# Latent attention by head pairs: products made one pair ahead, even rows written straight into SBUF, stores begun by three engines

## The chip, the cores and the metric

One core of a Trainium2 chip runs the whole network in one program. The metric is the device time of that program in microseconds (us). The engines are TensorE (PE in the tables; its weight loads are PEld), VectorE (DVE), ScalarE (ACT), GpSimd (POOL) and SyncE (SP, which here only begins DMAs). The trace of the kernel before comes from one profiled execution.

## The reference

Two layers work on 1280 tokens of width 1024 (256 context tokens, 1024 latent ones). A layer projects its input into three groups of heads, mixes them, projects back, and adds a gated convolutional feed-forward block. The change touches the third group, multi-head latent attention with eight heads:

```
cq  = rms_norm(p[9]);   q = cq @ w_uq          # rank 256 -> 8 heads x (64 plain + 32 rotated)
ckv = rms_norm(p[10]);  kn = ckv @ w_uk;  v = ckv @ w_uv     # rank 128 -> 8 heads x 64 each
kr  = p[11]                                    # 32 rotated key columns, one set for all heads
s = (qn . kn + qr . kr) * 96 ** -0.5           # latent queries: 1280 keys; context queries: 256
out = softmax(s) @ v
```

In layer 0 all 1280 tokens are queries, in layer 1 the 1024 latent ones (`lo` in the code is 0 or 256).

## The kernel before

Everything is kept transposed: features on partitions, tokens along the free dimension. Each float32 operand of a large product is split into a rounded high part (a cast on ScalarE, line 212) and a remainder (a subtraction on VectorE, line 213), both fp32r, and a product is three matmuls: high by high, high by low, low by high.

The attention is a Python generator, `mla`. It is woven with a second one, `lin`, which computes the two linear-attention groups: a serial pass over chunk states (lines 594 to 619, `lin_states`), then outputs by group. `weave` takes 1.1 steps of `lin` for each of `mla`, and a scheduler then sets the order of instructions on each engine. The first two steps of `mla` stand at the end of the second projection.

The stage has these parts. `first` makes the split weights, K of head pair 0 (`prod_k`), the rotated query columns of heads 0 to 3 (`prod_qr`), Q of pair 0, V of all heads (`prod_v`, line 872, 512 columns a matmul), and K of pairs 1 to 3. K and Q products (line 885) go through one of three PSUM banks, are split into `t` tiles, and are stored to DRAM (`kq`, line 930); V goes to DRAM too (`vm`, line 875). `load` (lines 942 to 944) then brings one head's K, Q and rotated Q into 96-partition tiles `Kt` and `Q`. While head 0 runs, `rest` makes Q of pairs 1 to 3 and the rotated columns of heads 4 to 7; while head h runs, `following` loads head h + 1.

A head works through query blocks of 128: nine score matmuls of up to 512 keys (`scores`, line 992), maxima on VectorE, exponentials on ScalarE (line 1005), ten transposes on TensorE (`turn`, line 1018), and the product with V (`values`, line 1042), whose normalization needs two diagonal tiles from GpSimd (line 1038). Scores use two sets of three banks in turn; products made meanwhile borrow the three banks of the other set. One output tile per head pair (`ob`) is stored in two pieces to `m` (line 1056). All DMAs are begun by SyncE, which works through its queue in order. Tiles come from pools with a fixed number of buffers: six `t`, sixteen `hid`, eight `h`, eight `y`, four `ws`.

Of the kernel before, what the change touches and what calls it, by code (L numbers as in the profile page):

```python
# [9 lines left out]
F32 = mybir.dt.float32  # L10
# [9 lines left out]
T = 1280  # L20
# [54 lines left out]
class Net:  # L75
# [754 lines left out]
    def mla(self, l, S):  # L830
# [14 lines left out]
        V, Q, ob = {}, {}, {}  # L845
# [6 lines left out]
        def weights():  # L852
            t = [self.hid([128, 512], F32R) for _ in range(2)]
            weight("r", a["uqr"][l].rearrange("p k n -> p (k n)"), [[x[:]] for x in t], 1)
# [10 lines left out]
        def prod_v():  # L865

            t = [self.hid([128, 512], F32R) for _ in range(2)]
# [8 lines left out]
            W.pop("v")  # L876

        def load_v(p):
            V[p] = [self.hid([128, 5, 128]) for _ in range(2)]
            for i in range(2):  # L880
                nc.sync.dma_start(V[p][i][:], S.vm[:, 5 * i:5 * i + 5, 128 * p:128 * p + 128])
# [5 lines left out]
        def prod_qr(x):  # L887

            terms = [(W["r"][wa][0][:, 256 * kc + 128 * x:256 * kc + 128 * x + 128], S.cq[kc][ca]) for kc in range(2) for wa, ca in order]
            for o in range(lo, T, 512):  # L890
# [19 lines left out]
            if x:  # L910
                W.pop("r")

        def prod_k(p):
            hs_ = slice(128 * p, 128 * p + 128)
            to_memory(p, 0, 0, [(W["k"][wa][0][:, hs_], S.ckv[ca]) for wa, ca in order])

        def prod_q(p):
            hs_ = slice(128 * p, 128 * p + 128)
            to_memory(p, 1, lo, [(W["n"][wa][kc][:, hs_], S.cq[kc][ca]) for kc in range(2) for wa, ca in order])

        def to_memory(p, y, o0, terms):

            for o in range(o0, T, 512):
                n = min(512, T - o)
                t = bank()[:, 0:n]
                product(t, o, n, terms)
                hi, lw = self.tt([128, 512], F32R), self.tt([128, 512], F32R)
                self.split(hi[:, 0:n], lw[:, 0:n], t)
                for x, s in enumerate((hi, lw)):
                    nc.sync.dma_start(S.kq[:, p, y, x, o:o + n], s[:, 0:n].bitcast(F32))  # L930
                del hi, lw, s

        def load(h):

            Q[h] = [self.hs([128, T]) for _ in range(2)]
            if h < 2:
                for b in range(2):
                    cs = slice(640 * b, 640 * b + 640)
                    self.split(Kt[h][0][64:96, cs], Kt[h][1][64:96, cs], S.kr[b][64:96, :])
            rows, rot = slice(64 * (h % 2), 64 * (h % 2) + 64), slice(32 * (h % 4), 32 * (h % 4) + 32)  # L940
            for x in range(2):
                nc.sync.dma_start(Kt[h % 2][x][0:64].bitcast(F32), S.kq[rows, h // 2, 0, x])
                nc.sync.dma_start(Q[h][x][0:64, lo:T].bitcast(F32), S.kq[rows, h // 2, 1, x, lo:T])
                nc.sync.dma_start(Q[h][x][64:96, lo:T].bitcast(F32), S.qr[rot, h // 4, x, lo:T])

        def first():
            weights()
            prod_k(0)
            yield
            prod_qr(0)  # L950
            prod_q(0)
            load(0)
            yield
            prod_v()
            yield
            for p in (1, 2, 3):
                prod_k(p)
            load_v(0)
            S.ckv.clear()
            yield  # L960

        def rest():
            load(1)
            S.kr.clear()
            prod_q(1)
            yield
            prod_q(2)
            yield
            prod_qr(1)
            yield  # L970
            prod_q(3)
            S.cq.clear()
            yield

        def following(h):
            load(h)
            if h % 2 == 0:
                load_v(h // 2)
            yield
# [50 lines left out]
        def values(h, qp, pts, sts, nk):  # L1030
# [19 lines left out]
            o = ob[h // 2]  # L1050
            for i in range(2):
                nc.vector.tensor_tensor(o[r:r + 64, 256 * qp + 128 * i:256 * qp + 128 * i + 128],  # L1052
# [5 lines left out]
        for _ in first():  # L1058
            yield
# [473 lines left out]
```

## Time and profile before

| | us |
|---|---|
| median of three runs | 3505.2 |
| lowest and highest run | 3504.65, 3507.97 |
| profiled execution, its own time | 3494.19 |
| its span, first to last instruction | 3492.3 |
| TensorE busy | 3363.4 (96%) |
| VectorE busy | 2225.3 (64%) |
| ScalarE busy | 1549.2 (44%) |
| GpSimd busy | 399.4 (11%) |

Read it as an account of TensorE: what it does in order, and between which instructions it is idle. A wait is put down to the instruction that ended it. Rows of SyncE give the time for which beginning a DMA holds its queue, not the transfer.

### The profile page before, as it was taken

To read this page: it belongs to the slowest core of one execution; us is meant where nothing else is said; L and a number is where in the kernel's file an instruction comes from. 1 tells how busy PE (TensorE), PEld (TensorE's weight loads), DVE (VectorE), ACT (ScalarE), POOL (GpSimd) and SP (SyncE) were. 2 spreads that over 40 slices of the span, in tenths; PEclk is the share of its full clock that TensorE was granted. 3 is DMA by queue.
4 is the path that set the end of the run, shared out by engine and by line. 5 is a ranking of instruction groups with operands and counts; after the bars stand their busy time and mean duration, and the time that the engine had idled before them with its cause. 6 is when DMAs were issued, how large, how long until landed. Compare 5 with 4: busy or idle time off the path is not lost.

```text
span 3492.3 us, 58230 instructions
## 1 busy us (share of the span) xinstructions
PE 3363.4 (96%) x23310; PEld 2932.7 (84%) x23310; DVE 2225.3 (64%) x3797; ACT 1549.2 (44%) x2881; POOL 399.4 (11%) x627
## 2 busy tenths in 40 slices
PE   8997899999999999999999998899999999999998
PEld 6996677678999999999999997577777888888897
DVE  3434678876774444675557844688877765586555
ACT  3333555554453332343334543555554544345433
POOL 0000244441010000000000000134310010001001
PEclk9998899999999999999999998899999999999999
DMA  7656522234223333432223445532234333223321
GB/s 291 202 176 199 200 77 77 62 92 145 73 73 117 119 121 126 152 103 73 79 73 117 168 135 180 188 84 78 57 101 127 99 94 97 92 95 115 96 92 49
DMA packets 207311, 410.01 MB, mean 117 GB/s; under 512 B 18176, under 2 KB 108096, under 8 KB 207040
## 3 DMA queue, kind: packets, MB, share of 16 engines
q1 hardware_dynamic: 207040, 406.29, 36.8%
q8 instruction: 183, 3.00, 0.4%
q14 instruction: 88, 0.72, 0.1%
HBM read 339.90 MB, written 66.32 MB: 116 GB/s over the span
## 4 chain that ended last, share of the span: by engine, by line
PE 84%; DVE 8%; DMA 3%; ACT 2%; issue 2%; SPq 0%; POOL 0%; DVEq 0%; POOLq 0%; ACTq 0%
PE ps L323 45%; PE ps L1242 16%; PE ps L992 5%; PE ps L1042 3%; PE ps L1018 3%; PE ps L457 3%; PE ps L263 1%; PE ps L647 1%; DVE sm L994 1%; DVE hid L707 1%; PE ps L651 1%; PE ps L885 1%; DMA ws<-in_ada_dram 1%; DVE hid L697 1%; ACT w L1005 1%
## 5 line engine op out<-in xcount | busy, mean ns | idle before, releaser
L323 PE MATMUL ps<-h,w 128*128 128x320 f32 (+5 forms) x9600 | 1664.8, 334 | 12.8 <-ACT h L212 6.3
L323 PEld LDWEIGHTS ps<-h,w 128*128 128x128 f32 x9600 | 1530.6, 189 | 144.2 <-issue 7.1
L213 DVE TENSOR_TENSOR w<-ws,w 128x1024 fp32r<-128x1024 f32 x360 | 441.1, 1226 | 564.7 <-PE ps L323 288.6
L1242 PE MATMUL ps<-hid,w 128*128 128x256 f32 (+4 forms) x3696 | 577.2, 316 | 1.5 <-ACT hid L212 1.4
L1242 PEld LDWEIGHTS ps<-hid,w 128*128 128x128 f32 x3696 | 539.6, 189 | 36.0 <-issue 7.6
L212 ACT CAST w<-ws 128x1024 fp32r<-128x1024 f32 x360 | 379.0, 1054 | 419.5 <-PE ps L1242 291.6
L992 PE MATMUL ps<-h,h 96*128 96x512 f32 (+1 forms) x1200 | 330.3, 395 | 31.6 <-DVE w L1020 11.3
L992 PEld LDWEIGHTS ps<-h,h 96*128 96x128 f32 x1200 | 198.7, 194 | 89.3 <-issue 21.5
L1209 DVE SCALAR_TENSOR_TENSOR t<-u,vec,t 128x642 f32<-128x642 f32 (+3 forms) x176 | 144.6, 822 | 181.6 <-ACT t L1208 181.5
L1203 ACT COPY u<-ps 128x512 f32<-128x512 f32 (+4 forms) x264 | 118.3, 483 | 312.1 <-PE ps L323 312.1
L1005 ACT ACTIVATE w<-ps,sm 128x768 f32<-128x768 f32 (+2 forms) x272 | 208.6, 773 | 101.9 <-DVE sm L1001 78.3
L1247 DVE SCALAR_TENSOR_TENSOR y<-ps,mod,y 128x320 f32<-128x320 f32 (+5 forms) x376 | 197.2, 558 | 68.1 <-PE ps L1242 67.7
L1018 PE MATMUL ps<-ident,w 128*128 128x128 f32 x1312 | 224.7, 287 | 13.1 <-ACT w L1005 12.8
L1038 POOL TENSOR_SCALAR dg<-ident,sm 128x128 f32<-128x128 f32 x144 | 98.9, 690 | 995.0 <-DVE sm L1036 906.4
L1018 PEld LDWEIGHTS ps<-ident,w 128*128 128x128 f32 x1312 | 155.0, 144 | 66.9 <-issue 29.1
L1199 POOL MEMSET u<- 128x1 f32 (+1 forms) x264 | 20.8, 102 | 1613.8 <-DVE t L1210 1436.3
L1042 PE MATMUL ps<-w,hid 128*64 128x128 f32 x2624 | 195.2, 282 | 7.3 <-DVE y L1052 7.1
L994 DVE TENSOR_REDUCE sm<-ps 128x1 f32<-128x1024 f32 x128 | 156.3, 1222 | 58.4 <-PE ps L992 48.4
L1042 PEld LDWEIGHTS ps<-w,hid 128*64 128x64 f32 x2624 | 150.5, 138 | 47.2 <-issue 29.1
L1022 ACT COPY w<-ps 128x256 f32<-128x256 f32 (+1 forms) x272 | 128.0, 473 | 109.4 <-PE ps L1018 106.6
L720 POOL TENSOR_TENSOR hid<-hid,hid 128x512 f32<-128x512 f32 x108 | 147.3, 1381 | 68.1 <-ACT hid L700 48.0
L1208 ACT ACTIVATE t<-u,vec 128x642 f32<-128x642 f32 (+3 forms) x176 | 153.6, 872 | 0.4
(197 smaller groups left out, 3231.8 us busy)
## 6 DMA issues: line engine op xcount, KB each, us to landing
ws<-in_up_dram SPq DMA_DIRECT2D x176, 512.0 KB, 3.6
ws<-in_down_dram SPq DMA_DIRECT2D x88, 512.0 KB, 3.4
ws<-in_ada_dram SPq DMA_DIRECT2D x80, 512.0 KB, 4.9
ws<-in_w_in_dram SPq DMA_DIRECT2D x48, 512.0 KB, 4.3
kq<-t SPq DMA_DIRECT2D x64, 256.0 KB, 2.5
ws<-in_w_out_dram SPq DMA_DIRECT2D x32, 512.0 KB, 3.7
h<-kq SPq DMA_DIRECT2D x48, 320.0 KB, 5.2
y<-in_ada_dram SPq DMA_DIRECT2D x16, 512.0 KB, 8.2
```

The costliest lines, as they stand in the source:

```text
L212: self.nc.scalar.copy(hi, src)
L213: self.nc.vector.tensor_tensor(lo, src, hi.bitcast(F32), op=ALU.subtract)
L323: nc.tensor.matmul(ps[:, i, 0:n], w_[:, k, :], h[k][:, part, o:o + n], start=(k == 0 and q == 0), stop=(k == 7 and q == 2))
L720: nc.gpsimd.tensor_tensor(X[n][:], blk(E[n][:, 0, cs[i]]), qx[:], op=ALU.mult)
L992: nc.tensor.matmul(sc[:, o:o + n], q[qa][0:96, qs], K[ka][0:96, o:o + n], start=(x == 0), stop=(x == 2))
L994: nc.vector.tensor_reduce(st[:, 1:2], sc[:, 0:1024], axis=AX.X, op=ALU.max)
L1005: nc.scalar.activation(P[:, c0:c1], sc[:, c0:c1], AF.Exp, bias=st[:, 2:3], scale=MSCALE, accum_out=st[:, 3 + j:4 + j])
L1018: nc.tensor.transpose(ps[:, t_], P[:, 128 * (t0 + t_):128 * (t0 + t_) + 128], self.ident[:])
L1042: nc.tensor.matmul(op[64 * i:64 * i + 64, 0], V[h // 2][t_ // 5][:, t_ % 5, r:r + 64], pts[i][:, t_], start=(t_ == 0), stop=(t_ == nk - 1) ...
L1208: nc.scalar.activation(v[:, 0:n], u[:, 1:1 + n], AF.Identity, scale=cw(j, 1), bias=self.vec[l][:, V_CB + j:V_CB + j + 1])
L1242: nc.tensor.matmul(pb[i][:, 0:n], w[w_][:, x, ms], p.hh[f0 + x][hp][:, o - 1:o - 1 + n], start=(x == 0 and q == 0), stop=(x == gn - 1 and ...
L1247: nc.vector.scalar_tensor_tensor(t, pb[i][:, o:o + n], self.md(l, 5, m, who), t, op0=ALU.mult, op1=ALU.add)
```

## The change

K, Q and V of a head pair are now made while the odd head before that pair runs (pair 0 ahead of head 0), each in a step of its own: `prod_kq` (two steps) and `prod_v` (one). The product tile of a pair has the even head's 64 rows on top and the odd head's below. The top half goes by DMA straight into the even head's `Kt[0]` or `Q` tile, and the bottom half to DRAM, from where `load` brings it during the even head. The high parts' DMAs are begun by ScalarE, the remainders' by GpSimd. V of a pair is computed as ten 128x128 blocks into three banks and copied into its SBUF tiles, with no trip through DRAM. The weights of `prod_qr` and `prod_v` are loaded and split by 128 columns (`some`). Outputs go to a `t` tile for each head and 256 queries, and each is stored at once by SyncE. The diff, with `...` where lines are left out:

```diff
-        def prod_v():
-
-            t = [self.hid([128, 512], F32R) for _ in range(2)]
-            weight("v", a["ukv"][l][:, 1], [[x[:]] for x in t], 1)
+        def some(src, n):
+
+            raw, t = self.tt([128, n, 128]), self.hid([128, 2, n, 128], F32R)
+            nc.sync.dma_start(raw[:], src)
+            self.split(t[:, 0], t[:, 1], raw[:])
+            return t
+
+        def prod_v(p):
+            w = some(a["ukv"][l][:, 1:2, 128 * p:128 * p + 128], 1)
+            V[p] = [self.hid([128, 5, 128]) for _ in range(2)]
+            b = flip[0] ^ 3
+            ps = self.ps[:, b:b + 3, :].rearrange("p a b -> p (a b)")
             for t_ in range(10):
-                p = bank()
                 for x, (wa, ca) in enumerate(order):
-                    nc.tensor.matmul(p, S.ckv[ca][:, 128 * t_:128 * t_ + 128], W["v"][wa][0], start=(x == 0), stop=(x == 2))
-                s = self.tt([128, 512])
-                nc.scalar.copy(s[:], p)
-                nc.sync.dma_start(S.vm[:, t_, :], s[:])
...
+                    nc.tensor.matmul(ps[:, 128 * t_:128 * t_ + 128], S.ckv[ca][:, 128 * t_:128 * t_ + 128], w[:, wa, 0],
+                                     start=(x == 0), stop=(x == 2))
             for i in range(2):
-                nc.sync.dma_start(V[p][i][:], S.vm[:, 5 * i:5 * i + 5, 128 * p:128 * p + 128])
+                nc.scalar.copy(V[p][i][:].rearrange("p a b -> p (a b)"), ps[:, 640 * i:640 * i + 640])
+            yield
...
-                for y, s in enumerate((hi, raw)):
-                    nc.sync.dma_start(S.qr[:, x, y, o:o + n], s[:, 0:n].bitcast(F32))
+                for y, (s, eng) in enumerate(((hi, nc.scalar), (raw, nc.gpsimd))):
+                    eng.dma_start(S.qr[:, x, y, o:o + n], s[:, 0:n].bitcast(F32))
...
+        def prod_kq(p):
+
+            h = 2 * p
+            Q[h] = [self.hs([128, T]) for _ in range(2)]
...
+            turned(h)
             hs_ = slice(128 * p, 128 * p + 128)
+            for y in range(2):
...
+                for o in range(lo if y else 0, T, 512):
+                    n = min(512, T - o)
+                    t = bank()[:, 0:n]
+                    product(t, o, n, terms)
+                    parts = [self.tt([128, 512], F32R) for _ in range(2)]
+                    self.split(parts[0][:, 0:n], parts[1][:, 0:n], t)
+                    for x, (s, eng) in enumerate(zip(parts, (nc.scalar, nc.gpsimd))):
+                        eng.dma_start((Q[h] if y else Kt[0])[x][0:64, o:o + n].bitcast(F32), s[0:64, 0:n].bitcast(F32))
+                        eng.dma_start(S.kq[:, p, y, x, o:o + n], s[64:128, 0:n].bitcast(F32))
+                    del parts, s
+                yield
+
+        def load(p):
+
+            h = 2 * p + 1
             Q[h] = [self.hs([128, T]) for _ in range(2)]
...
+                nc.sync.dma_start(Kt[1][x][0:64].bitcast(F32), S.kq[:, p, 0, x])
+                nc.sync.dma_start(Q[h][x][0:64, lo:T].bitcast(F32), S.kq[:, p, 1, x, lo:T])
...
-            if h % 2 and qp in (2, 4):
-                c0, c1 = (lo, 768) if qp == 2 else (768, T)
-                nc.sync.dma_start(S.m[:, 4 + h // 2, c0:c1], o[:, c0:c1])
...
+            nc.sync.dma_start(S.m[r:r + 64, 4 + h // 2, 256 * qp:256 * qp + 256], o[r:r + 64])
...
+        weights()
+        for _ in chain(prod_qr(0), prod_kq(0), prod_v(0)):
             yield
...
             if h % 2 == 0:
-                ob[h // 2] = self.yk()
-            side = rest() if h == 0 else following(h + 1) if h < 7 else iter(())
+                side = load(h // 2)
+            elif h < 7:
+                p = (h + 1) // 2
+                side = chain(*[prod_qr(1)] * (p == 2), prod_kq(p), prod_v(p))
```

How instructions move, in three places of layer 0. First TensorE, where V's products end. Before, these rows are the last V product (`L872`, all eight heads wide), the rest of a chunk of the linear attention's states (`L612`), and K of pair 1 (`L885`, `y` being the compressed keys and `ws` the weights):

```order
L872 MATMUL ps<-hid_3155,y_374 128x512
L612 MATMUL ps<-hid_3135,hid_3152 32x64 x4
L885 MATMUL ps<-y_374,ws_2576 128x512
L885 MATMUL ps<-y_375,ws_2576 128x512
L885 MATMUL ps<-y_374,ws_2576 128x512 x2
L885 MATMUL ps<-y_375,ws_2576 128x512
L885 MATMUL ps<-y_374,ws_2576 128x512
L885 MATMUL ps<-y_374,ws_2576 128x256
```

Now the end of V's products of pair 0 alone (`L877`) is followed at once by scores of head 0 (`L968`, which was line 992):

```order
L877 MATMUL ps<-hid_3185,y_374 128x128
L877 MATMUL ps<-hid_3185,y_373 128x128
L968 MATMUL ps<-h_2565,h_2709 128x256
L968 MATMUL ps<-h_2565,h_2710 128x256
L968 MATMUL ps<-h_2566,h_2709 128x256
L968 MATMUL ps<-h_2565,h_2709 128x512
L968 MATMUL ps<-h_2565,h_2710 128x512
L968 MATMUL ps<-h_2566,h_2709 128x512
```

K of pair 1 has gone from here into head 1.

Then ScalarE. Before, in head 0, the casts of the products (`L212`) stand by themselves among exponentials (`L1005`), chunk work (`L734`, `L700`, `L703`) and copies of transposes (`L1022`):

```order
L212 CAST t_3714<-hid_3703 128x256
L212 CAST t_3806<-ps 128x512
L212 CAST t_3818<-ps 128x512
L212 CAST t_3830<-ps 128x256
L1005 ACTIVATE w_3754,sm_3719<-ps,sm_3719 128x512
L1005 ACTIVATE w_3754,sm_3719<-ps,sm_3719 128x768
L734 COPY t_3911<-ps 128x512
L700 ACTIVATE hid_4047<-hid_4046 128x2x64x2
L703 ACTIVATE hid_4047<-hid_4046 128x64x2
L1022 COPY w_3846<-ps 128x512
L703 ACTIVATE hid_4047<-hid_4046 128x64x2
```

Now, in head 1, two DMAs stand behind each cast, one into the even head's tile (`L942`) and one to DRAM (`L943`); `L981` is the exponentials, `L998` the copies of transposes:

```order
L981 ACTIVATE w_3943,sm_3900<-ps,sm_3900 128x512
L981 ACTIVATE w_3943,sm_3900<-ps,sm_3900 128x768
L212 CAST t_3975<-ps 128x512
L998 COPY w_4015<-ps 128x512
L942 DMA h_2565<-t_3975 64x512
L943 DMA kq_372<-t_3975 64x512
L212 CAST t_3986<-ps 128x512
L653 COPY hid_4021<-ps 128x2x128
L942 DMA h_2565<-t_3986 64x512
L943 DMA kq_372<-t_3986 64x512
L212 CAST t_3997<-ps 128x256
L998 COPY w_4015<-ps 128x256
```

Up to the next exponential there are eight DMAs in this place.

Last GpSimd. Before, in the same part of the stage, it holds diagonal tiles (`L1038`, for the normalization) and the linear attention's products (`L716`, `L720`, `L803`) only:

```order
L1038 TENSOR_SCALAR dg_4082<-ident,sm_3836 128x128
L1038 TENSOR_SCALAR dg_4086<-ident,sm_3893 128x128
L1038 TENSOR_SCALAR dg_4157<-ident,sm_3963 128x128
L1038 TENSOR_SCALAR dg_4161<-ident,sm_4041 128x128
L716 TENSOR_TENSOR hid_4209<-u_3738,hm 128x512
L720 TENSOR_TENSOR hid_4219<-hid_4010,hid_4209 128x512
L720 TENSOR_TENSOR hid_4237<-hid_4036,hid_4209 128x512
L1038 TENSOR_SCALAR dg_4291<-ident,sm_4103 128x128
```

Now, in head 1, twelve DMAs stand between two pairs of diagonal tiles (`L1014`). The six for K are left out here; these are the six for Q, and what stands behind them:

```order
L942 DMA h_3969<-t_4082 64x512
L943 DMA kq_372<-t_4082 64x512
L942 DMA h_3969<-t_4096 64x512
L943 DMA kq_372<-t_4096 64x512
L942 DMA h_3969<-t_4110 64x256
L943 DMA kq_372<-t_4110 64x256
L1014 TENSOR_SCALAR dg_4255<-ident,sm_3900 128x128
```

The diagonal tile in the last row now comes behind the remainders of a whole pair's K and Q.

## Rows read from the trace of the kernel before

**Rows 1.** The page, parts 1 and 2: busy time by engine; granted clock in 40 slices

```profile
PE 3363.4 (96%) x23310; PEld 2932.7 (84%) x23310; DVE 2225.3 (64%) x3797; ACT 1549.2 (44%) x2881; POOL 399.4 (11%) x627
...
PEclk9998899999999999999999998899999999999999
```

**Rows 2.** Stretches of 100 us; columns: stretch, length, busy time (count) by engine, clock, DMA

```profile
500.00:600.00 100.00, 96.33 (x848) 73.39 (x847) 80.88 (x177) 56.20 (x148) 44.21 (x45) 0.95 0.18 50
...
2400.00:2500.00 100.00, 94.94 (x847) 73.28 (x845) 84.43 (x169) 55.87 (x144) 36.66 (x35) 0.98 0.29 78
```

**Rows 3.** Stretches of 10 us around the first heads of both layers

```profile
330.00:340.00 10.00, 4.93 (x99) 3.53 (x88) 2.43 (x6) 2.70 (x10) 0.00 (x0) 0.50 1.07 220
...
400.00:410.00 10.00, 5.39 (x51) 3.60 (x51) 9.16 (x15) 2.74 (x7) 7.80 (x6) 0.83 0.56 177
410.00:420.00 10.00, 6.56 (x19) 5.06 (x20) 7.99 (x16) 5.51 (x15) 0.60 (x1) 0.52 0.57 195
...
2220.00:2230.00 10.00, 9.39 (x72) 7.80 (x73) 5.90 (x15) 7.27 (x21) 1.20 (x2) 0.69 0.62 201
```

**Rows 4.** Waits of TensorE from 354 to 420 us: total, times, longest

```profile
PE ps L992 <- DVE t L901: 6.2, 2, 4.0
PE ps L992 <- DVE t L213: 3.4, 3, 1.9
PE ps L885 <- DVE t L213: 1.6, 3, 0.8
```

**Rows 5.** Waits of TensorE from 2204 to 2264 us

```profile
PE ps L885 <- DVE t L213: 2.4, 4, 0.9
PE ps L992 <- DVE t L213: 1.7, 3, 0.7
PE ps L885 <- DVE w L1020: 0.8, 1, 0.8
PE ps L992 <- DVE t L901: 0.7, 1, 0.7
```

**Rows 6.** Groups by line and shape, TensorE: busy us, mean ns, idle before

```profile
L457 PE MATMUL ps<-w,h 128*128 128x256 f32 x960 | 116.7, 281 | 0.0
...
L647 PE MATMUL ps<-hid,hid 128*128 128x128 f32 x272 | 47.3, 293 | 1.9 <-DVE hid L640 1.8
...
L872 PE MATMUL ps<-hid,y 128*128 128x512 f32 x60 | 17.1, 449 | 0.0
```

**Rows 7.** TensorE in order of time, four transposes and a single one: start, length

```profile
705.56 0.27 PE L1018 MATMUL ps<-ident,w 128*128 128x128 f32 x1
...
709.03 0.60 PE L1018 MATMUL ps<-ident,w 128*128 128x128 f32 x4
```

**Rows 8.** SyncE's issues of line 930: ns least, median, most

```profile
L930 SPq DMA_DIRECT2D kq<-t x88: 319/398/1816, 282.2 to 2268.4; - x88
```

**Rows 9.** What the transposes' weight loads (line 1018) waited for: us, times

```profile
  ACT w L1005: 21.3, 29
```

**Rows 10.** The page, part 5: a tensor operation on GpSimd

```profile
L720 POOL TENSOR_TENSOR hid<-hid,hid 128x512 f32<-128x512 f32 x108 | 147.3, 1381 | 68.1 <-ACT hid L700 48.0
```

**Rows 11.** SyncE's queue, layer 0, around the first head's loads

```profile
306.97 4.46 SPq L930 DMA_DIRECT2D kq<-t  x6
...
316.20 0.42 SPq L471 DMA_DIRECT2D gqk<-t  x1
316.67 0.43 SPq L588 DMA_DIRECT2D hid<-gqk  x1
```

**Rows 12.** ScalarE at the data of that store

```profile
312.14 0.44 ACT L469 ACTIVATE t<-ps 128x320 f32<-128x320 f32 x1
```

**Rows 13.** TensorE at head 0's first scores and the states' next chunk

```profile
321.52 0.66 PE L992 MATMUL ps<-h,h 96*128 96x256 f32 x2 [2.26 <-DMA h<-qr]
323.21 1.12 PE L604 MATMUL ps<-ident,hid 128*128 128x128 f32 x4 [1.03 <-DVE hid L597]
```

**Rows 14.** ScalarE, 500 to 800 us: exponentials of full score blocks

```profile
L1005 ACT ACTIVATE w<-ps,sm 128x768 f32<-128x768 f32 x43 | 38.5, 895 | 0.0
```

More of the change, by code (lines that the diff above doesn't have):

```diff
@@ L852, in weights @@
         def weights():
-            t = [self.hid([128, 512], F32R) for _ in range(2)]
-            weight("r", a["uqr"][l].rearrange("p k n -> p (k n)"), [[x[:]] for x in t], 1)
             t = self.ws([128, 2, 512], F32R)
@@ L887, in prod_qr @@
         def prod_qr(x):
-            terms = [(W["r"][wa][0][:, 256 * kc + 128 * x:256 * kc + 128 * x + 128], S.cq[kc][ca]) for kc in range(2) for wa, ca in order]
+            w = some(a["uqr"][l][:, :, 128 * x:128 * x + 128], 2)
+            terms = [(w[:, wa, kc], S.cq[kc][ca]) for kc in range(2) for wa, ca in order]
             for o in range(lo, T, 512):
@@ L917, in prod_q @@
[L917 to L931, printed above, removed]
@@ L946, in first @@
[L946 to L973, printed above, removed]
@@ L975, in following, with turned @@
[L975 to L978, printed above, removed]
+            del w, terms
+            yield
+        def turned(h):
+            for x in range(2):
+                nc.sync.dma_start(Q[h][x][64:96, lo:T].bitcast(F32), S.qr[32 * (h % 4):32 * (h % 4) + 32, h // 4, x, lo:T])
+        def prod_kq(p):
+            h = 2 * p
+            Q[h] = [self.hs([128, T]) for _ in range(2)]
+            if p == 0:
+                for K in Kt:
+                    for b in range(2):
+                        cs = slice(640 * b, 640 * b + 640)
+                        self.split(K[0][64:96, cs], K[1][64:96, cs], S.kr[b][64:96, :])
+                S.kr.clear()
+            turned(h)
+            hs_ = slice(128 * p, 128 * p + 128)
+            for y in range(2):
+                if y:
+                    terms = [(W["n"][wa][kc][:, hs_], S.cq[kc][ca]) for kc in range(2) for wa, ca in order]
+                else:
+                    terms = [(W["k"][wa][0][:, hs_], S.ckv[ca]) for wa, ca in order]
+                for o in range(lo if y else 0, T, 512):
[8 more added lines that the diff above has]
+                    del parts, s
+                yield
@@ L1049, in values, with chain @@
             nc.scalar.copy(rb[:], op[:, 1])
-            o = ob[h // 2]
+            o = self.tt([128, 256])
             for i in range(2):
-                nc.vector.tensor_tensor(o[r:r + 64, 256 * qp + 128 * i:256 * qp + 128 * i + 128],
+                nc.vector.tensor_tensor(o[r:r + 64, 128 * i:128 * i + 128],
                                         op[64 * i:64 * i + 64, 0], rb[64 * i:64 * i + 64, :], op=ALU.mult)
-            if h % 2 and qp in (2, 4):
-                c0, c1 = (lo, 768) if qp == 2 else (768, T)
-                nc.sync.dma_start(S.m[:, 4 + h // 2, c0:c1], o[:, c0:c1])
-        for _ in first():
+            nc.sync.dma_start(S.m[r:r + 64, 4 + h // 2, 256 * qp:256 * qp + 256], o[r:r + 64])
+        def chain(*gs):
+            for g in gs:
+                yield from g
+        weights()
+        for _ in chain(prod_qr(0), prod_kq(0), prod_v(0)):
             yield
@@ L1348 @@
         S.qr = net.dp.tile([128, 2, 2, T], F32, name=f"qr{l}")
-        S.kq = net.dp.tile([128, 4, 2, 2, T], F32, name=f"kq{l}")
-        S.vm = net.dp.tile([128, 10, 512], F32, name=f"vm{l}")
+        S.kq = net.dp.tile([64, 4, 2, 2, T], F32, name=f"kq{l}")
         S.ckv = [net.yk(F32R) for _ in range(2)]
```

21 lines of the change are left out of this document (3 added, 18 removed).

## The prediction

> **What bounds the kernel now.** Read the page's busy line and its clock line first: TensorE is busy 96% of the span, ScalarE 44%, GpSimd 11%, and the granted clock leaves its upper level (2.4 GHz) in only a few slices [rows 1]. So the time is TensorE's work plus what it loses, and a change that keeps its matmuls moves the time only through lost stretches, or through what a matmul costs. The table by stretches says what bounds the attention stage, the only one touched: in a typical 100 us of it TensorE is 96% busy, VectorE 80%, ScalarE 56%, GpSimd 44% in layer 0 and 37% in layer 1 [rows 2]. The 10 us slices show where TensorE loses most: while the linear attention's states go round serially (330 to 340 us: 4.9 of 10 us busy, clock 0.50), and again where head 0 runs beside the other pairs' products (410 to 420 us, and 2220 to 2230 us with its clock at 0.69) [rows 3]. The waits of TensorE in those second stretches name the cause: VectorE's splits and rotations (lines 213, 901), with VectorE itself 9.2 of 10 us busy from 400 to 410 us [rows 3 to 5].
>
> **The change, part by part.** The sum is made against the profiled execution (3494.2 us); the three timed runs have their median 11 us above it, and I add the same difference to both.
>
> *V products.* Before, 60 matmuls of 512 columns (30 a layer) take 17.1 us, 0.285 us each [rows 6]. Now there are 240 of 128 columns, each with its own weight load. The trace has no fp32r matmul of 128 columns. Its nearest rows: 960 fp32r matmuls of 256 columns at 116.7/960 = 0.122 us, half of which, 0.061, is the price if time follows columns alone; four transposes of 128 columns end 0.60 us after the first begins, against a single one's 0.27 us, so one each 0.11 us; and plain f32 records of 128 columns take 47.3/272 = 0.174 us [rows 6, 7]. I take 0.115 us, next to the transposes and to the 256-column row, because a weight load of 128 columns stands in front of each: 240 x 0.115 = 27.6, so +10.5 us. Ends: 240 x 0.061 = 14.6 (-2.5) and 240 x 0.174 = 41.8 (+24.7). The Trainium skill's "TensorE: Matmul & The Clock Gate", section "Back-to-back issue gap", gives about 81 ns for sustained matmul and weight-load pairs of 128 columns; by that the term would be an estimated +2.3 us, but the 256-column row here stands 0.015 us above its columns' share, so I stay with the rows.
>
> *Products moved.* K and Q of pairs 1 to 3 and the second rotation (7 steps a layer) leave the stretch around head 0 and go, in the same number of matmuls, into heads 1, 3 and 5, where V's products of those pairs join them: 10 steps a layer. In the old places their splits cost TensorE 6.2 + 3.4 + 1.6 = 11.2 us in layer 0 and 2.4 + 1.7 + 0.8 + 0.7 = 5.6 us in layer 1 [rows 4, 5]: 16.8 us for 14 steps, 1.2 us each. These waits go; late next in the same banks are the splits in the new places. There VectorE is 80% busy and not 92%, so I take 0.9 us: 20 x 0.9 = 18.0, net +1. Ends: nothing at all (-17), or 1.6 us a step, layer 0's price (+15). The clock comes back too: at 0.83 and 0.52 over 5.4 and 6.6 busy us, and at 0.69 over 9.4 [rows 3], the old stretches lost 0.9 + 3.1 + 2.9 = 7 us. I book -7; 0 if the new place cools it as much.
>
> *ScalarE begins 98 stores* (54 in layer 0, 44 in layer 1). On SyncE such an issue holds the queue 0.32 us at least, 0.40 at the median and 1.8 at most [rows 8]. 27 of them fall ahead of the heads, beside projections and states; 71 stand between the exponentials of heads 1, 3 and 5: 71 x 0.40 = 28 us of ScalarE. Each waits for ScalarE's own cast, so the exponentials behind it wait too, and the transposes behind those. ScalarE's 44% of idle time hides the rest, but in 29 of the 144 score blocks (80 in layer 0, 64 in layer 1) the transposes' weight loads already stood waiting for an exponential [rows 9]. So I charge 29/144 of 28 us: +6. Ends 0 and 28.
>
> *GpSimd begins 98 more.* No row of before has one. The nearest are SyncE's 0.40 us and a 128x512 tensor operation on GpSimd, 1.38 us [rows 8, 10]: 71 x (0.40 to 1.38) = 28 to 98 us of an engine that is over half idle. Behind them wait the diagonal tiles (line 1038) that the end of a head's values needs, and the split tiles' six buffers. I take +4, ends 0 and 53 (the second rival).
>
> *The start.* SyncE's queue: six K/Q stores from 306.97 us, six loads, and only at 316.20 us the store of gqk, whose data ScalarE had finished at 312.58 us; its reload is issued at 316.67 us [rows 11, 12]. That holds up the states' next chunk at 323.21 us [rows 13]. With the stores and even rows gone, three loads still stand ahead of it. I take -2 a layer, -4 in all; ends 0 and -7. It can't be more, since TensorE's own queue waits for the rotated rows until 321.52 us anyway [rows 13], and they still go through memory.
>
> *Outputs and the rest.* 72 small output stores replace 16 large ones: 56 more issues of 0.40 us on SyncE, which loses 88 K/Q stores, 20 stores and 16 loads of V. Costed at nothing: SyncE's queue has room. If that cover goes, the output tiles hold the same six buffers as the splits, and VectorE waits.
>
> Sum: +10.5 + 1 - 7 + 6 + 4 - 4 = **+10.5 us**: 3505 us in a profiled execution, and 3505.2 + 10.5, about **3516 us**, as the median.
>
> **Rivals.** *The start gets short.* Around head 0 the products went through three banks with VectorE nearly full; without them head 0 may run like a later head. Then the 16.8 us of waits and 7 us of clock do not come back, since the scheduler has transposes and linear attention to put behind each product, ScalarE's issues hide in its idle time, and the start's -4 holds: -17 - 7 - 4 + 10.5 = -17.5, **3488 us**. For it: VectorE's load in the heads is lower than at 400 us. Against: one engine order runs both, and 10 steps now stand where 7 stood.
>
> *GpSimd runs late.* A pair's two product steps bring 12 issues within two score blocks; 43 full blocks in 300 us make a block 7.0 us [rows 14], so 14 us, of which GpSimd already uses 44%, 6.2 us. Above (14 - 6.2)/12 = 0.65 us an issue, stores fall behind, the split tiles stay held, and products, banks and scores follow. At 1.38 us it is 12 x 1.38 - 7.8 = 8.8 us a pair, six pairs, 53 us; if the blocks behind catch up half, +26 in place of my +4: **3538 us**. The Trainium skill's "SBUF — State Buffer", section "SBUF: two separate sides", speaks for it: descriptors of a transfer begun by GpSimd are written by GpSimd, and a VectorE copy in its two-port mode locks it out. No run here shows that, and most VectorE work of these heads reads PSUM.
>
> *Nothing measurable:* a V product at 0.061 us, ScalarE's issues hidden, steps and clock even: within a few us of 3505.
>
> **How the numbers follow.** Chances: the forecast (above +7 us) 0.38, GpSimd late 0.13, short start 0.31, nothing 0.18. About 0.2% (7 us) is what a measurement of this kernel can tell from no change. So slower 0.51, same 0.18, faster 0.31. The range goes from the short start, with a little more, to the late GpSimd, with half of V's upper end: 3484 to 3550; the forecast's own is 3512 to 3530.
>
> **What would show it.** V's matmuls (new line 877) at 0.11 to 0.12 us each, 240 of them, confirm the largest term; under 0.07 or over 0.17 refutes it. TensorE's waits on line 213's splits should appear in heads 1, 3 and 5 and be gone around head 0, where the clock should stay up. ScalarE's queue should show about 0.4 us an issue, and the transposes' waits for exponentials should grow past 21 us and 29 times. If GpSimd's issues exceed 0.65 us and matmuls wait for its tiles or diagonals, the second rival is at work. The forecast is wrong if the attention stretches of both layers get shorter in sum.

## The result and the profile after

The changed kernel takes 3546.97 us as a median (3539.91 to 3550.99, 4 runs), and the kernel before, measured beside it, 3504.93 us: 1.0117 of before, 95% interval 1.0098 to 1.0135. So it is 42 us slower, where 10.5 were forecast. In the profiled executions the span grows by 54.7 us, from 3492.3 to 3547.0. The 12.6 us between the two figures are no work: the profiled execution of before was 10.7 us quicker than its median, that of the changed kernel 1.9 us slower than its own. What follows is told against the profiles, one execution of each kernel.

The page of the changed kernel, its busy line, its clock line and its DMA queues (q1 is begun by SyncE, q10 by ScalarE, q0 by GpSimd):

```profile
span 3547.0 us, 58820 instructions
...
PE 3408.4 (96%) x23490; PEld 2977.6 (84%) x23490; DVE 2217.4 (63%) x3805; ACT 1548.7 (44%) x2885; POOL 448.2 (13%) x725
...
PEclk9997998999999999999999998899899999999999
...
q1 hardware_dynamic: 180672, 361.19, 32.7%
q10 hardware_dynamic: 8480, 12.33, 1.2%
q0 software_dynamic: 4576, 12.33, 1.2%
```

Against [rows 1], TensorE is busy 45.0 us longer and idle only 9.7 us longer. A longer busy time has two sources: more work, or the same work at the lower clock. They are told apart with the granted clock: over slices of some 10 us, busy time times (1 - clock) is what the lower level took. That sum is 45.2 us before and 76.8 us after. So the 54.7 us are **9.7 of idle time, 31.6 lost to the lower clock, and 13.4 of work**. (In slices of 100 us both sums come out some 15 us higher, and they differ by 30.6.) By place: 18.6 us up to the end of layer 0's attention and 31.6 in layer 1's; most of the other 4.5 us stand behind the last matmul of the program, where 12.2 us have become 16.6, and are idle time of TensorE in code that the change did not touch.

How much of this is chance between two executions, the other runs can say, since each has its mean granted clock. Span times (1 - clock), idle time included, is 70 us in the profiled execution of before and 106 in that of the changed kernel, 36 more. Over all runs on record it averages 74 to 76 us before (four sets of runs) and 98 for the changed kernel: some 24 us more, beside a slowdown of 42. So the lower clock is no accident of one execution, but the two profiles make it look larger than it is.

Three stretches of 100 us of the changed kernel (columns as in [rows 2]; the clock stands behind the engines), and the last two of them in the kernel before; its first is in [rows 2]:

```profile
500.00:600.00 100.00, 90.46 (x655) 68.53 (x654) 66.94 (x143) 45.25 (x115) 33.38 (x42) 0.88 0.28 81
2200.00:2300.00 100.00, 88.41 (x856) 69.21 (x856) 66.00 (x158) 50.62 (x144) 30.64 (x34) 0.82 0.24 67
2500.00:2600.00 100.00, 92.60 (x719) 70.69 (x718) 67.20 (x144) 46.51 (x117) 35.57 (x44) 0.86 0.40 120
```

```profile
2200.00:2300.00 100.00, 90.97 (x760) 68.38 (x759) 73.58 (x163) 55.06 (x143) 29.73 (x29) 0.97 0.57 184
...
2500.00:2600.00 100.00, 96.18 (x854) 73.67 (x855) 79.49 (x175) 55.85 (x139) 31.31 (x40) 0.98 0.29 92
```

VectorE and ScalarE are busy for less of the time than before, GpSimd for about as much, and the clock is 0.82 to 0.88 and not 0.95 to 0.98: TensorE is not held up by a fuller engine; it is idle for somewhat longer, and does its own work slower. Where, the groups by line say (busy us, mean ns | idle before), first for the scores, the transposes, the product with V and V's own products of the changed kernel, then for the first three before:

```profile
L968 PE MATMUL ps<-h,h 96*128 96x512 f32 (+1 forms) x1200 | 339.8, 404 | 32.1 <-DVE t L213 10.7 <-DVE w L996 8.3 <-DMA h<-t 5.3
...
L994 PE MATMUL ps<-ident,w 128*128 128x128 f32 x1312 | 228.0, 291 | 13.9 <-ACT w L981 13.7
...
L1018 PE MATMUL ps<-w,hid 128*64 128x128 f32 x2624 | 206.0, 286 | 8.5 <-DVE t L1028 5.9 <-ACT w L998 2.1
...
L877 PE MATMUL ps<-hid,y 128*128 128x128 f32 x240 | 43.9, 362 | 0.6 <-DVE hid L213 0.6
```

```profile
L992 PE MATMUL ps<-h,h 96*128 96x512 f32 (+1 forms) x1200 | 330.3, 395 | 31.6 <-DVE w L1020 11.3 <-DVE t L901 6.9 <-DVE t L213 5.1
...
L1018 PE MATMUL ps<-ident,w 128*128 128x128 f32 x1312 | 224.7, 287 | 13.1 <-ACT w L1005 12.8
...
L1042 PE MATMUL ps<-w,hid 128*64 128x128 f32 x2624 | 195.2, 282 | 7.3 <-DVE y L1052 7.1
```

V's products (line 877) take 43.9 us for 240, 0.183 us each, 26.8 us more than the 17.1 of [rows 6]. Line 877 alone, in windows around five of its eight batches (TensorE busy and count, weight loads, clock, DMA share, GB/s):

```profile
339.00:349.00 10.00, 6.66 (x30) 6.47 (x30) 0.50 0.20 62
430.00:440.00 10.00, 3.78 (x30) 3.50 (x30) 1.00 0.01 2
700.00:710.00 10.00, 3.46 (x30) 3.50 (x30) 0.85 0.16 43
2440.00:2450.00 10.00, 6.80 (x30) 6.55 (x30) 0.52 0.05 11
2558.00:2568.00 10.00, 6.66 (x30) 6.48 (x30) 0.50 0.17 51
```

A batch of 30 takes 3.5 to 3.8 us at the upper level, 0.115 to 0.126 us each, and 6.7 to 6.8 us at the lower, 0.222 to 0.227. (The clock column is that of the whole window: in the third row it rose before the batch began.) Three batches of eight meet the upper level (from 431, 705 and 2311 us), five the lower, one of these (from 575 us, 6.3 us) for most of its length. How a batch gets there, the stretch around the last one shows (all engines, columns as in the three rows of 100 us):

```profile
2548.00:2558.00 10.00, 5.28 (x28) 3.67 (x28) 5.68 (x9) 4.78 (x15) 5.26 (x7) 0.58 0.85 295
2558.00:2568.00 10.00, 10.00 (x45) 8.55 (x42) 1.63 (x4) 2.13 (x5) 1.37 (x2) 0.50 0.17 51
2568.00:2578.00 10.00, 10.00 (x68) 7.86 (x66) 6.64 (x15) 2.48 (x6) 5.02 (x5) 0.55 0.34 109
```

First TensorE idles 4.7 of 10 us and the clock falls to its lower level; then V's step follows, and TensorE is busy without a gap for 20 us at 0.50 to 0.55. Read in slices of 2 us, the changed kernel has 16 low stretches between 0 and 1000 and between 1900 and 2700 us, and the slice ahead of each had TensorE idle for 0.8 to 2.0 us. The five that meet a V batch last 12 to 46 us, most others 4 to 8.

What TensorE waited for, over the whole span (us in total, times, longest):

```profile
PE ps L994 <- ACT w L981: 13.7, 13, 4.0
PE ps L968 <- DVE t L213: 10.7, 9, 2.8
PE ps L604 <- DVE hid L597: 9.1, 4, 3.1
...
PE ps L612 <- ACT hid L606: 8.3, 13, 0.7
PE ps L604 <- DVE hid L599: 8.2, 7, 1.9
```

The splits (line 213) are waited for nine times; 10.5 of these 10.7 us lie in the four stretches 526 to 580, 676 to 716, 2424 to 2464 and 2534 to 2590 us, in heads 3 and 5. Around head 0, where [rows 4, 5] stood full of them, there is none.

The store issues (min/median/max ns), first on ScalarE, then on GpSimd, for the even rows and for the DRAM copy:

```profile
L942 ACTq DMA_DIRECT2D h<-t x44: 468/468/1425, 303.1 to 2545.5; - x44
...
L942 POOL DMA_DIRECT2D h<-t x44: 516/518/595, 304.1 to 2547.5; - x44
...
L943 ACTq DMA_DIRECT2D kq<-t x44: 453/609/1070, 298.6 to 2549.5; - x44
L943 POOL DMA_DIRECT2D kq<-t x44: 532/532/552, 299.6 to 2548.0; - x44
```

One place shows how such stores can hold up TensorE all the same (timeline: start, duration, engine, line; in brackets the idle time before and what ended it):

```profile
688.42 1.03 POOL L716 TENSOR_TENSOR hid<-u,hm 128x512 f32<-128x512 f32 x1
689.52 1.27 POOL L720 TENSOR_TENSOR hid<-hid,hid 128x512 f32<-128x512 f32 x1
690.74 0.58 POOL L942 DMA_DIRECT2D h<-t  x1
691.32 0.54 POOL L943 DMA_DIRECT2D kq<-t  x1
...
693.24 0.37 ACT L212 CAST t<-ps 128x256 fp32r<-128x256 f32 x1 [5.14 <-DMA kq<-t]
...
693.64 0.42 DVE L213 TENSOR_TENSOR t<-ps,t 128x256 fp32r<-128x256 f32 x1 [3.19 <-ACT t L212]
694.12 1.65 PE L968 MATMUL ps<-h,h 96*128 96x512 f32 x3 [2.85 <-DVE t L213]
```

GpSimd's two stores stand behind 2.3 us of its tensor work; the next cast has no free split tile until a store has landed, VectorE waits for the cast, and the scores for VectorE. The issue itself (0.54 to 0.58 us) is not what is late: the stores begin late, behind that work.

### The profile page after: what moved, and what is told of

Its sections match the earlier page's. It is cut to its first block, busy times and chain, and to the rows that moved or that the text cites. A ratio compares the mean times of both kernels' runs of the same rounds, so it can differ in the third digit from the quotient of the medians.

```text
span 3547.0 us, 58820 instructions
## 1 busy us (share of the span) xinstructions
PE 3408.4 (96%) x23490; PEld 2977.6 (84%) x23490; DVE 2217.4 (63%) x3805; ACT 1548.7 (44%) x2885; POOL 448.2 (13%) x725
## 4 chain that ended last, share of the span: by engine, by line
PE 85%; DVE 6%; DMA 3%; issue 2%; ACT 2%; POOL 0%; SPq 0%; ACTq 0%; DVEq 0%; POOLq 0%
PE ps L323 44%; PE ps L1224 15%; PE ps L968 5%; PE ps L1018 4%; PE ps L994 3%; PE ps L457 3%; PE ps L877 1%; PE ps L885 1%; PE ps L647 1%; PE ps L263 1%; DVE sm L970 1%; PE ps L651 1%; DMA ws<-in_ada_dram 1%; PE ps L354 1%; DVE hid L707 1%
## 5 line engine op out<-in xcount | busy, mean ns | idle before, releaser
L212 ACT CAST w<-ws 128x1024 fp32r<-128x1024 f32 x360 | 379.1, 1054 | 418.6 <-PE ps L1224 291.5
L968 PE MATMUL ps<-h,h 96*128 96x512 f32 (+1 forms) x1200 | 339.8, 404 | 32.1 <-DVE t L213 10.7
L968 PEld LDWEIGHTS ps<-h,h 96*128 96x128 f32 x1200 | 207.3, 202 | 90.2 <-issue 20.2
L1191 DVE SCALAR_TENSOR_TENSOR t<-u,vec,t 128x642 f32<-128x642 f32 (+3 forms) x176 | 144.6, 821 | 182.5 <-ACT t L1190 182.4
L981 ACT ACTIVATE w<-ps,sm 128x768 f32<-128x768 f32 (+2 forms) x272 | 209.0, 774 | 105.1 <-DVE sm L977 80.2
L1018 PE MATMUL ps<-w,hid 128*64 128x128 f32 x2624 | 206.0, 286 | 8.5 <-DVE t L1028 5.9
L998 ACT COPY w<-ps 128x256 f32<-128x256 f32 (+1 forms) x272 | 128.0, 474 | 120.3 <-PE ps L994 116.6
L720 POOL TENSOR_TENSOR hid<-hid,hid 128x512 f32<-128x512 f32 x108 | 144.2, 1352 | 86.4 <-ACT hid L700 58.6
L212 ACT CAST hid<-t 128x642 fp32r<-128x642 f32 (+5 forms) x100 | 63.5, 635 | 207.7 <-DVE t L1196 204.8
```

Of the source, the lines that this page charges most:

```text
L212: self.nc.scalar.copy(hi, src)
L968: nc.tensor.matmul(sc[:, o:o + n], q[qa][0:96, qs], K[ka][0:96, o:o + n], start=(x == 0), stop=(x == 2))
L981: nc.scalar.activation(P[:, c0:c1], sc[:, c0:c1], AF.Exp, bias=st[:, 2:3], scale=MSCALE, accum_out=st[:, 3 + j:4 + j])
L1018: nc.tensor.matmul(op[64 * i:64 * i + 64, 0], V[h // 2][t_ // 5][:, t_ % 5, r:r + 64], pts[i][:, t_], start=(t_ == 0), stop=(t_ == nk - 1) ...
L1191: nc.vector.scalar_tensor_tensor(v[:, 0:n], u[:, 0:n], cw(j, 0), v[:, 0:n], op0=ALU.mult, op1=ALU.add)
```

## The experiments

Theory A: V's thin products cost what the clock makes of them, and the odd heads, where they stand, are where the clock falls. Rivals: B, the stores of ScalarE and GpSimd; C, the K and Q products' own stalls. Ratios are to the kernel before, with 95% intervals; the split into idle, lower clock and work is that of one profiled execution each, worked out as above, and executions of one kernel lie up to 15 us apart. The last column is span times (1 - granted clock) as the mean of all runs of the kernel on record, which is the surer sign of the clock. The work column is coarse: five kernels with the same matmuls (before, V put back with either stores, stores alone, outputs alone) lie between 3311.8 and 3323.7.

| kernel | ratio | span | idle | lower clock | work | all runs |
|---|---|---|---|---|---|---|
| before | 1 | 3492.3 | 128.9 | 45.2 | 3318.2 | 74 to 76 |
| changed | 1.0117 | 3547.0 | 138.6 | 76.8 | 3331.6 | 98 |
| V put back | 1.0030 | 3504.7 | 136.4 | 44.6 | 3323.7 | 75 |
| V ahead of K, Q | 1.0156 | 3548.2 | 144.3 | 62.7 | 3341.2 | 93 |
| V alone on before | 1.0047 | 3514.8 | 130.6 | 48.6 | 3335.6 | 74 |
| V in even heads | 1.0042 | 3509.7 | 128.5 | 42.5 | 3338.7 | 74 |
| steps spaced | 1.0114 | 3540.4 | 144.6 | 52.1 | 3343.7 | 79 |

**V put back.** In the changed kernel V is made as before: 512 columns, through DRAM.

```diff
...
-        for _ in chain(prod_qr(0), prod_kq(0), prod_v(0)):
+        for _ in chain(prod_qr(0), prod_kq(0), prod_v()):
...
-                side = chain(*[prod_qr(1)] * (p == 2), prod_kq(p), prod_v(p))
+                load_v(p)
+                side = chain(*[prod_qr(1)] * (p == 2), prod_kq(p))
```

> The changed kernel with V alone put back: 60 matmuls of 512 columns beside the start, kept in DRAM, read back pair by pair. Theory A (V's thin products meet the clock at its lower level: 240 at 0.183 us, 43.9 us, against 17.1 before, and the stretch behind them stays low): 27 us of V go, and 5 to 10 us of the 31.6 us more that the changed kernel loses to the lower level: 3510 to 3515 us, 1.002 to 1.003 of before. Theory B (late stores of GpSimd hold the split tiles) and theory C (K and Q products stall in the odd heads whatever V does): only V's own term at the upper level goes, 10.5 us, and some of its surplus: 3530 to 3537 us, 1.007 to 1.009.

3511.62 us, 1.003 (1.002 to 1.004): as theory A said. 32.2 of the 42.3 us that the profile loses are lower clock (in the last column, 98 against 75). Three quarters of the slowdown need V by pairs; B and C alone don't make it.

**All stores by SyncE.**

```diff
-                for y, (s, eng) in enumerate(((hi, nc.scalar), (raw, nc.gpsimd))):
+                for y, (s, eng) in enumerate(((hi, nc.sync), (raw, nc.sync))):
...
-                    for x, (s, eng) in enumerate(zip(parts, (nc.scalar, nc.gpsimd))):
+                    for x, (s, eng) in enumerate(zip(parts, (nc.sync, nc.sync))):
```

> The changed kernel with all 196 stores begun by SyncE again; all else as changed. Theory B: TensorE's waits on the splits (10.7 us, 9 times) shrink, since no store stands behind GpSimd's 1.27 us products any more, and the clock stays up where they went: 10 to 20 us less than the changed kernel, 3527 to 3537 us. Theories A and C: within 7 us of the changed kernel, 3540 to 3554 us.

1.0102 (1.0087 to 1.0117), in between, and TensorE's waits on the splits are as in the changed kernel (10.1 us, 8 times): B is not what makes the 42 us. The place at 688 us is real, but without GpSimd a wait stays there: at 700 us the same scores wait 2.1 us, once more for a split tile that a store still holds, now a store of SyncE. The run tells against theory A too. Five of the six V batches of the odd heads run at the upper level here, and line 877 takes 36.6 us and not 43.9; the kernel gains only 5 us by it all. So what V's own products lose to the clock in these heads is a small part of the 42 us.

**V ahead of K and Q** in heads 1, 3 and 5.

```diff
-                side = chain(*[prod_qr(1)] * (p == 2), prod_kq(p), prod_v(p))
+                side = chain(*[prod_qr(1)] * (p == 2), prod_kq(p))
+                side = chain(prod_v(p), side)
```

> The changed kernel with V's step put ahead of the K and Q steps of its head (1, 3, 5). Theory A, if the K and Q steps' stalls lower the clock and V only comes after them: V's products of those heads run at 0.115 us as at 704 us, the 9 us that three of these batches pay at the lower level go, with some us behind them: 3530 to 3540 us. If the thin products themselves lower the clock: no gain, 3543 to 3555 us, and the clock falls at V's place in the new order too.

1.0156 (1.014 to 1.0172): the worst. Line 877 alone in this kernel, two of its batches (columns as above):

```profile
680.00:690.00 10.00, 3.56 (x30) 3.42 (x30) 1.00 0.52 168
2410.00:2420.00 10.00, 3.86 (x30) 3.51 (x30) 1.00 0.59 183
```

All six batches of the odd heads now run at the upper level, so the thin products do not lower the clock by themselves. And yet nothing is gained: the lower clock still takes 62.7 us, nearly half of it in the two stretches at the start of the stages and most of the rest in short ones among the odd heads' scores, transposes and values, and the idle time grows. My simple form of theory A, that V only pays for where it stands in the queue, falls here.

**V alone on the kernel before**, by pairs, in heads 1, 3 and 5 of a kernel whose K and Q are made around head 0.

```diff
...
             load(h)
+            yield
             if h % 2 == 0:
-                load_v(h // 2)
-            yield
+                yield from prod_v(h // 2)
```

> The kernel before with V alone changed: ten 128-column blocks a pair, made in heads 1, 3 and 5 (pair 0 at the start), copied straight to SBUF. Theory A with the K and Q steps as what lowers the clock: V at 0.115 us each, +10.5 us, the clock as before: 3512 to 3518 us, 1.002 to 1.004. If the thin products lower the clock by themselves: V above 0.16 us each and colder stretches in heads 1, 3, 5: 3525 to 3540 us, 1.006 to 1.010.

1.0047 (1.0033 to 1.0061), 3515.62 us against 3500.66, +15: the ratio lies a little above A's. V takes 35.2 us, the clock costs 3.4 us more than before. The same products in the same heads that cost about 30 us in the changed kernel cost half of that where K and Q are not there. (That kernel also stores and loads as before; but with all stores by SyncE, V by pairs costs still more beside K and Q, 1.0102 against 0.9993, so the stores are not what makes the difference.)

**V of the next pair in the even heads** of the changed kernel.

```diff
-                side = load(h // 2)
+                side = chain(load(h // 2), *([prod_v(h // 2 + 1)] if h < 6 else []))
...
-                side = chain(*[prod_qr(1)] * (p == 2), prod_kq(p), prod_v(p))
+                side = chain(*[prod_qr(1)] * (p == 2), prod_kq(p))
```

> The changed kernel with V of the next pair made in the even head before (0, 2, 4), so that the odd heads hold K and Q only, as in the run with V put back, and V stands where it has no K or Q step beside it. Theory A2 (V's thin products cost their columns and some us each alone, +16 us as in the kernel before with V by pairs, and the rest of the +31 us comes from standing in one head with K and Q): 3511 + 16, 3524 to 3532 us, 1.007 to 1.009. Theory V (the thin products cost 30 us wherever they stand): 3540 to 3552 us.

3519.11 us, 1.0042 (1.0029 to 1.0054), below what I expected. With the same products in another head, 0.0075 or 26 us of the 42 go. The same three stretches as above, in this kernel:

```profile
500.00:600.00 100.00, 90.41 (x742) 66.81 (x742) 75.69 (x166) 50.72 (x131) 44.82 (x52) 0.97 0.35 98
2200.00:2300.00 100.00, 95.79 (x844) 75.89 (x836) 72.39 (x166) 52.98 (x142) 38.91 (x41) 0.90 0.18 51
2500.00:2600.00 100.00, 94.91 (x785) 71.26 (x782) 76.79 (x165) 53.44 (x134) 36.66 (x49) 0.97 0.46 139
```

The clock is back at 0.97 in the first and the last; the 0.90 in the middle is pair 0's batch at the start of layer 1's stage. By the table, 34 us less are lost to the lower clock, and 10 us less are idle; this profiled execution was 7.7 us quicker than its kernel's median, but the last column says the same of the clock, 74 us and not 98.

**Steps spaced.** An empty step behind each K and Q step.

```diff
+        def spaced(g):
+            for _ in g:
+                yield
+                yield
...
-                side = chain(*[prod_qr(1)] * (p == 2), prod_kq(p), prod_v(p))
+                side = chain(*[prod_qr(1)] * (p == 2), spaced(prod_kq(p)), prod_v(p))
```

> The changed kernel with an empty step behind each K and Q step of pairs 1 to 3, so that in heads 1, 3 and 5 the steps run K, -, Q, -, V over five half-blocks instead of K, Q, V over three. Theory of crowding (three steps back to back each take the banks that the next scores need; stalls follow each other, and the clock stays at its lower level): most of what moving V to the even heads saved (28 us) is saved here too, 3520 to 3530 us, 1.005 to 1.008, with fewer low stretches in these heads. Theory of the head (what V costs is set by the head that holds it, its stores and copies beside K and Q's, not by the step just ahead): 3540 to 3550 us.

1.0114 (1.0095 to 1.0133): crowding of neighbouring steps is refuted. The clock did come back (52.1 us, V's products 34.9 us; over all runs 79 us, near the 74 to 76 of before), but idle time and work took its place. So the lower clock is where the time shows in the changed kernel, and not by itself what costs it: here the clock is nearly that of before, and the kernel is as slow. What TensorE waited for most, with V in the even heads, spaced, and with V ahead (one row of each):

```profile
PE ps L994 <- ACT w L981: 12.3, 18, 2.3
```

```profile
PE ps L994 <- ACT w L981: 17.8, 21, 2.6
```

```profile
PE ps L994 <- ACT w L981: 21.0, 17, 4.3
```

With V in the odd heads, in whatever place, the transposes wait 5 to 9 us longer for exponentials once V itself no longer runs low.

**A third of V.** The changed kernel with one of V's three terms for pairs 1 to 3, so 120 of the 240 matmuls are left out.

```diff
-                for x, (wa, ca) in enumerate(order):
+                some_ = order[:1] if p else order
+                for x, (wa, ca) in enumerate(some_):
...
-                                     start=(x == 0), stop=(x == 2))
+                                     start=(x == 0), stop=(x == len(some_) - 1))
```

> The changed kernel with only the first of V's three terms for pairs 1 to 3: 60 matmuls a layer at 128 columns left out, 120 of 240 in all; weight loads, splits, banks and copies stay. If the thin matmuls at the lower clock are the cost: 120 x 0.115 = 14 us at least, at 0.22 each 26 us, and some of the stretch behind: 3515 to 3528 us, 1.004 to 1.007. If the step itself is (banks, copies, the split of its weights) and the columns hardly matter: 14 us at most, 3533 to 3545 us.

3530.27 us, 1.0082 (1.0069 to 1.0096): 17 us less than changed, between the two expectations. V's row falls by 20.5 us to 23.4, so the columns matter, but more than half of the slowdown stays with a third of the matmuls. In the profile 15.2 us of lower clock go as well; over all runs hardly any does (95 us against 98).

**V in the even heads, pair 0's ahead of rotations, K and Q.**

```diff
-        for _ in chain(prod_qr(0), prod_kq(0), prod_v(0)):
+        for _ in chain(prod_v(0), prod_qr(0), prod_kq(0)):
...
```

> V in the even heads, and pair 0's V ahead of the rotations, K and Q at the start of the stage. In every run so far that batch stood in the low stretch of the start and took 6.7 us a layer against 3.5 at the upper level. If it comes before that stretch: 6 us less than with V in the even heads, about 3513 us, 1.002 to 1.003. If the start's stretch is set by the serial states alone and TensorE waits there anyway: no change, 3516 to 3522 us.

3521.38 us, 1.0059 (1.0045 to 1.0072): nothing gained. In layer 1 the batch still stood partly low (2150 to 2158 us), and the V batch of head 0 now fell into low stretches (362 to 380 and 2238 to 2258 us).

**Stores alone, outputs alone, and the pairs with SyncE.** Two single parts put on the kernel before, and two versions that join what helped: V put back with SyncE, V in the even heads with SyncE. The main lines of the first:

```diff
...
-                for x, s in enumerate((hi, lw)):
-                    nc.sync.dma_start(S.kq[:, p, y, x, o:o + n], s[:, 0:n].bitcast(F32))
+                for x, (s, eng) in enumerate(((hi, nc.scalar), (lw, nc.gpsimd))):
+                    eng.dma_start(S.kq[:, p, y, x, o:o + n], s[:, 0:n].bitcast(F32))
```

> The kernel before with nothing changed but who begins the K, Q and rotated stores: high parts ScalarE, remainders GpSimd, 54 and 54 of them in all. By the prediction's +6 and +4 for 98 each: some +5 us, 1.000 to 1.003. By rival two (GpSimd's tiles held): 1.004 to 1.010.

> The kernel before with the outputs alone changed: a tile of the split's pool for each head and 256 queries, stored at once by SyncE, in place of one tile a pair. By the prediction nothing: 0.999 to 1.001. If these tiles crowd the six that the splits need: 1.002 to 1.005, with VectorE waiting for tiles whose store is not yet done.

> V put back and the remaining stores begun by SyncE. If the store engines cost what the run with SyncE alone showed (1.0117 to 1.0102, about 5 us): 3503 to 3508 us, 1.000 to 1.002. If the 1.003 left with V put back is the moved K and Q products alone: no change, 3509 to 3515 us.

> V of the next pair in the even heads, and all stores begun by SyncE: the changed kernel with the two pieces put elsewhere that helped. SyncE in place of ScalarE and GpSimd gave 0.0015 with V in the odd heads (1.0117 to 1.0102) and 0.0037 with V put back (1.003 to 0.9993). If the two pieces add: 1.0042 less 0.0015 to 0.0037, 1.0005 to 1.0027, 3503 to 3511 us; so not faster than before, since the thin products' own work of 10 to 15 us stays. If SyncE's gain depends on V wide: no change, 1.004.

Stores alone 1.0011 (1.0001 to 1.002), outputs alone 0.9991 (0.9982 to 1.0001): both as predicted. V put back with SyncE 0.9993 (0.9984 to 1.0002), 0.0037 below the same kernel with the new stores; V in the even heads with SyncE 1.0027 (1.0017 to 1.0036), 0.0015 below. So the stores cost 4 to 13 us, the moved K and Q products and the even rows neither cost nor gain, and no version is measurably faster than before.

## Why the prediction was right in sign and short in size

The measured 3547 us lies in the stated range, 3484 to 3550, and outside the forecast's own, 3512 to 3530. That it lies in the wide one is luck: the range reached up there for a late GpSimd and half of V's upper end, and GpSimd is not what made the 42 us (with all stores by SyncE the kernel still stood at 1.0102).

**The step that failed** is "The clock comes back too ... I book -7; 0 if the new place cools it as much". Both ends were too low: the lower clock took 31.6 us more, 6.1 of it in layer 0's stage, 21.5 in layer 1's, and the rest outside them (over all runs the growth is smaller, about 24 us by span). The low stretches around head 0 did go, but the start's stretches grew (14.1 and 15.5 us lost, against 9.9 and 9.3, with pair 0's batch at the lower level in full), and heads 3 and 5 got longer ones; head 1 hardly did (1.7 and 1.5 us lost). I had counted what the clock had cost in the places that the products left, and given the places that they went to no price of their own, though a V batch there follows two steps for which I had charged 0.9 us of stall each. What that place costs, the runs give: V by pairs costs 0.0087 of the time, 30 us, in the odd heads and 0.0012, 4 us, in the even ones (1.0117 and 1.0042 against 1.0030 with V put back); with all stores by SyncE 0.0109 and 0.0034 (1.0102 and 1.0027 against 0.9993). The spaced steps show that these 26 us are not the clock alone, since they stay when the clock comes back.

**V products: +10.5 predicted, +26.8 in their own row.** The price of 0.115 us was right at the upper level, and the refutation that I had set (over 0.17) was met because five batches of eight stood at the lower. The price of the old products was also taken with the clock left out: in layer 0, 11 of the 30 wide ones took 3.83 us in a window in which the clock rose, and the 19 behind them 4.65 us at the upper level, 0.245 each (line 872 of the kernel before, columns as above):

```profile
340.00:350.00 10.00, 3.83 (x11) 3.06 (x12) 0.55 0.17 48
350.00:360.00 10.00, 4.66 (x21) 3.44 (x19) 1.00 0.96 362
```

At the upper level they would be 60 x 0.245 = 14.7 us and the thin ones 240 x 0.117 = 28, a difference of 13 us without the clock, which is also the work that the accounting above finds (13.4). V alone on the kernel before measured +15. The Trainium skill's "TensorE: Matmul & The Clock Gate", section "Back-to-back issue gap", has about 81 ns for such pairs; by the rows here it is 115 to 126 ns at the upper level and 222 to 227 at the lower, so the rows were the better guide, and neither is any use without the level.

**Products moved: +1.** Right, and for the reason given: the waits on splits and rotations left head 0 (16.8 us by [rows 4, 5]) and came up elsewhere (10.7 us on splits, nearly all in heads 3 and 5, and 3.7 on rotations). Idle time in the two stages grew by 0.5 and 3.7 us. The short start was half right: head 0 did get short (from its first score to its last 78 us and not 115 in layer 0, 73 and not 107 in layer 1), and the odd heads took it back.

**ScalarE +6, GpSimd +4.** The stores cost 4 us alone and 5 to 13 us beside the moved products: the size was right, the way only partly. The transposes' weight loads wait more often, and hardly longer, for an exponential than in [rows 9]:

```profile
PEld ps L994 <- ACT w L981: 23.9, 39, 4.3
```

GpSimd's issues take 0.52 to 0.58 us at the median, below the 0.65 at which my second rival decides. The Trainium skill's "SBUF — State Buffer", section "SBUF: two separate sides", lets a VectorE operation in a two-port mode keep GpSimd from writing a transfer's descriptors; the 44 issues of line 942 lie between 516 and 595 ns, and no run here shows such a hold.

**The start -4.** The transposes and products of the states' chunks (lines 604 and 612) wait 25.6 us, against 30.2 before: -4.6, as priced. It drowned in the low clock of the same stretch. **Outputs 0**: confirmed by a run of its own.

**What stays open.** V's step costs some 26 us more in the odd heads than in the even ones (1.0117 against 1.0042, and with all stores by SyncE 1.0102 against 1.0027, the same difference again), and some 15 more than in the odd heads of the kernel before, where K and Q are not made there. It is not the order (V ahead was slower), not the distance between the steps (spacing changed nothing), and not the columns alone (a third of them left 1.0082). In each of these kernels the time is made of idle time and lower clock together, in changing shares, and the waits go to the exponentials when the clock comes back. That the odd heads are full, so that any third step costs what it cannot hide, is what I would guess; no run shows which engine or buffer makes them so. Nothing was run with more buffers for the split tiles, or with another order of the linear attention beside these heads; neither is ruled out.

## What to carry to other kernels

A price taken from the trace holds for the clock at which its rows stood: read the granted clock beside each duration, and when a change splits wide products into thin ones behind a stall, price them at both levels and ask which one the new place has. When a step is moved, charge the place it goes to as well as crediting the one it leaves: here the stalls moved at an even price, and what TensorE lost to its lower level grew from 45 to 77 us in the profiles. Where runs carry their granted clock, read it in all of them before a profile's share is taken for the kernel's. A falling clock can be the sign and not the cause: one kernel here had it back and was as slow. And try the same work in a neighbouring place before giving up a change: one line of order was worth 26 of the 42 us.

## What the runs showed of the hardware

In the changed kernel products of 128 columns, each with its own weight load, took 0.115 to 0.126 us at the upper clock level and 0.222 to 0.227 at the lower, so nearly the whole factor of two; products of 512 columns in the kernel before 0.245 us at the upper, and 0.35 on average over the 11 during which the clock rose. In none of the batches that began at the lower level behind K and Q at the start of a stage (6.7 us each, in eight kernels) did the clock rise before the batch had ended. A DMA begun by GpSimd held that engine for 0.52 to 0.58 us at the medians of its lines, 0.77 at most, one begun by ScalarE for 0.33 to 0.61 us, with 1.43 us at most.
